# Taking matmul columns alternately from halves and quarters in 13 feature blocks of a feed-forward layer

## The chip, the core and the metric

The kernel runs on one core of a Trainium2 chip. Its engines work side by side, each on a queue of its own: TensorE (PE in the profile; its weight loads are listed apart as PEld) multiplies matrices, VectorE (DVE) and ScalarE (ACT) do elementwise work, GpSimd (POOL) a few small operations, and SyncE (SP) issues the loads of weights. Operands lie in SBUF, sums of matmuls in the eight banks of PSUM, 512 float32 columns each. The metric is the device time of one execution in microseconds (us); lower is better.

## The reference

Two layers, each a mixer followed by a SwiGLU feed-forward part, over 256 tokens with 1024 features, and a norm at the end. The change lies in the feed-forward part of layer 0:

```python
def swiglu(h, w13, w2):
    g, u = jnp.split(h @ w13, 2, axis=-1)
    return ((jax.nn.silu(g) * u) @ w2).astype(h.dtype)

for layer in range(DEPTH):
    y = rms_norm(h, norm_mix[layer])
    ...
    h = h + y
    h = h + swiglu(rms_norm(h, norm_ffn[layer]), ffn_w13[layer], ffn_w2[layer])
```

D_FF is 2816, so that `h @ w13` has 2 x 2816 output features: 22 blocks of 128 for the gate half g and as many for the half u. Inputs and outputs are float32.

## The kernel before

**Precision.** TensorE takes the operands as float32r. To keep the accuracy each operand is split into a high and a low part (`whi`, `wlo` for weights, `xh`, `xl` for activations, `hh`, `hl` for the hidden ones), and every product is three matmuls: high by high, low weights by high, high weights by low. `mm_w` (line 479) issues these three, with 128 x 128 weights as the stationary operand and 256 columns (all tokens) as the moving one, onto the same 256 columns of a PSUM bank. `mm` (line 454) is the helper behind all matmuls but the transposes, so that they all carry line 455 in the profile.

**Layout.** Features stand on the partitions, tokens along them. The activations x of layer 0's feed-forward part are eight pairs of tiles of 128 x 256, one pair per block k of input features.

**The feed-forward part** (`swiglu`, called with layer 0 and the bank group "A", so its sums are `psA`). Blocks 0 to 3 of the output features run together over the input blocks k. Then comes a loop over j from 4 to 21, one output block at a time (lines 997 to 1001):

```python
            b = main_bank(gu)
            for half in range(2):
                for k in range(KT):
                    mm_w(b[:, half * S:half * S + S], piece("ffn_w13", layer, k, half * DFF + P * j, P), x[k],
                         start=(k == 0 and half == 0), stop=(k == KT - 1))
```

The gate half fills columns 0 to 255 of the bank, the u half columns 256 to 511: 2 x 8 x 3 = 48 matmuls of 256 columns. `hidden(j, b)` then queues on VectorE and ScalarE what turns the bank into the hidden block (`sgq`, `u`, `hh`, `hl`), and `down(j - 4, hs)` runs the down projection of an earlier hidden block, 8 x 3 = 24 matmuls onto four banks of group "B" (`psB`), whose moving operand is `hh` and `hl`. So TensorE alternates between 48 matmuls onto `psA` and 24 onto `psB`. The tiles `hh0` and `hl0` take the place of `q1` and `k1` of the recurrence, which are laid out 304 columns wide with pads of 16 columns; the other hidden tiles are 256 wide.

**Weights** arrive by SyncE's loads of 512 KB into `raw`; ScalarE rounds them to `whi` (line 412) and VectorE subtracts to get `wlo` (line 414), each into a ring of six buffers, which come free as TensorE moves on.

**The order** of all engines' instructions is made while the program is built, by `Order`: it keeps a model clock for each engine, `od.main(MM)` advances TensorE's by 109.2 ns for each matmul, and `od.pump()` emits the queued operations that are due. The change leaves these calls as they are.

**The recurrence's level matmuls** of layer 0's mixer (`level` in `Core.scores`) are the place where the kernel before takes moving columns in pieces: of 128 columns of q it takes m, leaves m, and so on, with m of 2, 4, 8 and 16, 64 columns in all, against 128 - m columns of k. They write their columns side by side. `mov,k` are the recurrence's matmuls with 192 columns, taken side by side.

Of the kernel before, what the change touches and what calls it, by code (L numbers as in the profile page):

```python
# [20 lines left out]
KT = D // P  # L21
# [6 lines left out]
SUB = 1024  # L28
FIRST = (512, 512, 512, 512)
LEVELS = (1, 2, 4, 8, 16)  # L30
BUCKET_STARTS = tuple(range(17)) + (21, 27, 35, 46, 59, 77, 99, 128, 166, 216)


# [249 lines left out]
def cv(n, fast=False):  # L283
    return ((n / 2 if fast else n) + 66) / 0.96


def ca(n, ptr=0):
    return n / 1.2 + 93 + 93 * ptr
# [14 lines left out]
def hybrid_trunk(ctx: ExitStack, tc: tile.TileContext, wts, xT, par, gfin, tab, onehot, masks, out):  # L303
# [15 lines left out]
    def new(tag, shape, bufs=1, dt=FT, held=False):  # L319
        return ring(tag, shape, bufs, dt).new(held)  # L320
# [37 lines left out]
    def bank(g, held=False):  # L358
        return rings["ps" + g].new(held)

    def main_bank(g):

        b = bank(g, held=True)
        r = b.ring
        od.need(lambda: od.free_at(r))
        b.tile = r.make()
        r.past.append(b)
        return b
# [7 lines left out]
    def wrote(b):  # L376
        b.writers = [Mark(od.now)]
# [56 lines left out]
    def piece(name, layer, k, c0, n):  # L434
        assert plan[ws["piece"]] == (name, layer, k, c0, n), (plan[ws["piece"]], (name, layer, k, c0, n))
        ws["piece"] += 1
        if ws["col"] == subs[ws["sub"]][2]:
            ws["sub"] += 1
            ws["col"] = 0
            if keep["from"] is None:  # L440
                free_subs(ws["sub"])
        i, c = ws["sub"], ws["col"]
        make_subs(i + NSUB + 4)
        ws["col"] += n
        return Piece(i, c, n)

    def free_subs(upto):
        for j in range(max(0, upto - 12), upto):
            if hi_b[j].held:
                hi_b[j].held = lo_b[j].held = False  # L450
                hi_b[j].readers.append(Mark(od.now))
                lo_b[j].readers.append(Mark(od.now))

    def mm(o, a, b, start=False, stop=False):
        T.matmul(o, a, b, start=start, stop=stop, skip_group_check=True)  # L455
# [20 lines left out]
                b.held = False  # L476
                b.readers.append(Mark(od.now))

    def mm_w(o, w, x, start=False, stop=False):
        mm(o, w.hi, x.hi, start=start)  # L480
        od.main(MM)
        mm(o, w.lo, x.hi)
        od.main(MM)
        mm(o, w.hi, x.lo, stop=stop)
        od.main(MM, 1)
        od.pump()

# [33 lines left out]
    for k0, k1 in [(k, k + 1) for k in range(4)] + [(4, 6), (6, 8)]:  # L521
        od.op("S", 60, lambda k0=k0, k1=k1: nc.sync.dma_start(hT[:, k0:k1, :], xT[:, k0:k1, :]),  # L522
              writes=hb[k0:k1], nbytes=131072 * (k1 - k0), due=8 * k0 - 6)
    NMK = 2 * P + 64 * 2 * len(LEVELS)
    bt = new("bt", [P, NH * S])
# [90 lines left out]
    def out_rows(name, layer, k, us, banks, nk, done):  # L616

        if k == nk - 2:
            return
        ks = (k - 1, k) if k == nk - 1 else (k,)  # L620
        for j in range(KT):
            b, s = banks[j // 2], (j % 2) * S
            for kk in ks:
                mm_w(b[:, s:s + S], piece(name, layer, kk, P * j, P), us[kk], start=(kk == 0 and j % 2 == 0),
                     stop=(kk == nk - 1))
            if k == nk - 1 and j % 2:
                wrote(b)
                done(j // 2)
                b.held = False
        for kk in ks:  # L630
            us[kk].free()
# [21 lines left out]
    def feature_major(name, layer, c0, x, g):  # L653
        b = main_bank(g)
        for k in range(KT):
            mm_w(b[:, :S], piece(name, layer, k, c0, P), x[k], start=(k == 0), stop=(k == KT - 1))
        wrote(b)
        b.held = False
        return b
# [64 lines left out]
    class Core:  # L724
# [91 lines left out]
        def scores(self, due):  # L816
            h, Q, K, mov = self.h, self.Q, self.K, self.mov
            pm = pms[h % 2]
            moff = {m: 2 * P + P * i for i, m in enumerate(LEVELS)}

# [78 lines left out]
    for h in range(NH):  # L899
        c = Core(h)  # L900
# [46 lines left out]
    def swiglu(layer, x, stats, gu, down):  # L947

        hs = {}

        def hidden(j, b):
            gs = new("sgq", [P, S], 3)
            sg = new("u", [P, S], 3)
            due = 6
            od.op("V", cv(S), lambda: V.tensor_tensor(gs.tile, b[:, :S], stats.row.tile, op=OP.mult),  # L955
                  reads=[b, stats.row], alloc=[gs], due=due)
            od.op("A", ca(S), lambda: A.activation(sg.tile, gs.tile, AF.Sigmoid), reads=[gs], alloc=[sg], due=due)  # L957
            od.op("V", cv(S), lambda: V.tensor_tensor(gs.tile, gs.tile, sg.tile, op=OP.mult), reads=[sg], writes=[gs], due=due)
            od.op("V", cv(S), lambda: V.tensor_tensor(sg.tile, b[:, S:], gs.tile, op=OP.mult), reads=[b, gs], writes=[sg],
                  due=due)  # L960
            x = X("h", j % 7)
            hi, lo = x.h, x.l
            od.op("A", ca(S), lambda: A.activation(hi.tile, sg.tile, AF.Copy), reads=[sg], alloc=[hi], due=due + 6)
            od.op("V", cv(S), lambda: V.tensor_tensor(lo.tile, sg.tile, hi.tile.bitcast(FT), op=OP.subtract),
                  reads=[sg, hi], alloc=[lo], due=due + 6)
            hs[j] = x

        bk = [main_bank(gu) for _ in range(4)]
        for k in range(KT - 2):
            w = {}  # L970
            keep["from"] = ws["sub"]
            for j in range(4):
                for half in range(2):
                    w[j, half] = piece("ffn_w13", layer, k, half * DFF + P * j, P)
                    o = bk[j][:, half * S:half * S + S]
                    mm(o, w[j, half].hi, x[k].hi, start=(k == 0 and half == 0))
                    od.main(MM)
                    mm(o, w[j, half].lo, x[k].hi)
                    od.main(MM, .67)
                    od.pump()  # L980
            for j in range(4):
                for half in range(2):
                    mm(bk[j][:, half * S:half * S + S], w[j, half].hi, x[k].lo)
                    od.main(MM, .33)
                od.pump()
            keep["from"] = None
            free_subs(ws["sub"])
        for j in range(4):
            for half in range(2):
                for k in (KT - 2, KT - 1):  # L990
                    mm_w(bk[j][:, half * S:half * S + S], piece("ffn_w13", layer, k, half * DFF + P * j, P), x[k],
                         stop=(k == KT - 1))
            wrote(bk[j])
            hidden(j, bk[j])
            bk[j].held = False
        for j in range(4, FTN):
            b = main_bank(gu)
            for half in range(2):
                for k in range(KT):
                    mm_w(b[:, half * S:half * S + S], piece("ffn_w13", layer, k, half * DFF + P * j, P), x[k],  # L1000
                         start=(k == 0 and half == 0), stop=(k == KT - 1))
            wrote(b)
            hidden(j, b)
            b.held = False
            od.written(stats.row)
            down(j - 4, hs)
        for k in range(KT):
            x[k].free()
        down(FTN - 4, hs, last=True)
# [10 lines left out]

    od.written(sto.row)
    swiglu(0, x1, st1, "A", down0)


# [191 lines left out]
    def down1(k, hs, last=False):  # L1216
# [23 lines left out]
        if not last:  # L1240
            hs[k].free()

    swiglu(1, x3, st3, "B", down1)
    od.flush()


def _constants():
# [3 lines left out]
    for i in range(384):  # L1251
# [3 lines left out]
        else:  # L1255
            onehot[sum(dist >= s for s in BUCKET_STARTS) - 1, i] = 1.0
    s = np.arange(P)[:, None]
    m = [np.tile(np.eye(P, dtype=np.float32), (1, 2))]
    for lv in LEVELS:
        t = np.arange(P).reshape(-1, 2, lv)[:, 1].reshape(1, -1)  # L1260
# [30 lines left out]
```

## Time and profile before

| | |
|---|---|
| time, median of 2 runs | 630.43 us (630.02 to 630.84) |
| span of the profiled execution, first to last instruction (its device time is not listed apart) | 629.2 us |
| weights read from HBM | 109.78 MB, 176 GB/s over the span |
| loop over j of layer 0's feed-forward part, from block 6's first matmul to block 21's | 192.15 to 314.71 us |
| TensorE, VectorE, ScalarE busy in that stretch | 122.56, 77.92, 56.97 us |

In the profile, PE rows are matmuls, and matmuls overlap in the pipeline, so what one costs is the distance between the starts of two that follow each other. A row of the order in time gives the start in us, the length in us, the engine, the line, the operation, out<-in, the stationary operand's shape, the moving one's, and a count. In the table of stretches each engine has its busy time and the number of its instructions, and then come the granted TensorE clock (1.00 is full), the busy share of the DMA engines and what they moved.

### The profile page before, as it was taken

The page shows a single profiled execution, that of the slowest core. Times are in us where ns is not written, and L with a number is a line of the kernel's source. Part 1 is how long each engine was busy: PE and PEld are TensorE (multiplying, and loading weights), DVE is VectorE, ACT ScalarE, POOL GpSimd, SP SyncE. Part 2 cuts the span into 40 slices and gives each one's busy share as a digit, 9 for nine tenths or more (in the row PEclk, how much of TensorE's full clock was granted, in tenths as well). Part 3 has the DMA queues.
Part 4 walks back from the last instruction along what each step waited for, and adds up shares of the span by engine and source line. Part 5 has one row for each costly group of instructions (what it writes and reads, how often), then busy time and mean ns, then how long its engine had stood idle before and what let it go on. Part 6 is the DMA issues. An engine that isn't in the chain of part 4 may idle for free.

```text
span 629.2 us, 12441 instructions
## 1 busy us (share of the span) xinstructions
PE 617.4 (98%) x4848; PEld 594.2 (94%) x4848; DVE 441.0 (70%) x800; ACT 364.2 (58%) x715; POOL 39.2 (6%) x74
## 2 busy tenths in 40 slices
PE   7999999999999999999999999999999999999995
PEld 5899999999999999999998899999899999999994
DVE  5898878877786666666659678866686666666653
ACT  6798888875564444444446566564674444444443
POOL 0132112200400000000000000000100000000003
PEclk9999999999999999999999999999999999999998
DMA  8964443534896666666653564445545665555501
GB/s 273 324 217 136 154 128 123 155 115 134 209 282 200 194 199 198 190 189 198 201 189 116 209 223 160 143 154 182 180 160 197 201 199 197 177 188 176 168 1 67
DMA packets 32135, 111.83 MB, mean 178 GB/s; under 512 B 3835, under 2 KB 4508, under 8 KB 32076
## 3 DMA queue, kind: packets, MB, share of 16 engines
q1 hardware_dynamic: 31052, 108.71, 53.4%
q0 software_dynamic: 448, 1.25, 1.0%
q10 hardware_dynamic: 576, 1.08, 0.6%
q8 instruction: 38, 0.62, 0.4%
q14 instruction: 21, 0.17, 0.1%
HBM read 109.78 MB, written 1.25 MB: 176 GB/s over the span
## 4 chain that ended last, share of the span: by engine, by line
PE 78%; issue 16%; DVE 3%; DMA 1%; ACT 1%; POOL 1%; SPq 0%; ACTq 0%; DVEq 0%; POOLq 0%
PE psB L455 44%; PE psA L455 33%; DMA raw<-in_w_dram 1%; DVE wlo L414 1%; POOL ny L591 1%; DVE xl L541 0%; DVE yt L607 0%; ACT whi L412 0%; DVE hT L609 0%; DVE sqacc L559 0%; PE psB L1146 0%; SPq L401 0%; SPq L522 0%; PE psA L596 0%; DVE raw L1177 0%
## 5 line engine op out<-in xcount | busy, mean ns | idle before, releaser
L414 DVE TENSOR_TENSOR wlo<-raw,whi 128x1024 fp32r<-128x1024 f32 (+1 forms) x206 | 247.8, 1213 | 107.8 <-ACT whi L412 107.4
L412 ACT ACTIVATE whi<-raw 128x1024 fp32r<-128x1024 f32 (+1 forms) x205 | 213.0, 1050 | 145.7 <-issue 66.7
L455 PE MATMUL psB<-xh,whi 128*128 128x256 f32 x608 | 172.6, 287 | 0.0
L455 PE MATMUL psB<-xh,wlo 128*128 128x256 f32 x608 | 167.6, 279 | 0.0
L455 PE MATMUL psB<-xl,whi 128*128 128x256 f32 x608 | 163.3, 279 | 0.0
L455 PE MATMUL psA<-xh,whi 128*128 128x256 f32 x544 | 150.3, 280 | 0.0
L455 PE MATMUL psA<-xh,wlo 128*128 128x256 f32 x544 | 148.8, 277 | 0.0
L455 PE MATMUL psA<-xl,whi 128*128 128x256 f32 x544 | 144.0, 277 | 0.0
L455 PEld LDWEIGHTS psB<-xh,wlo 128*128 128x128 f32 x608 | 114.6, 188 | 0.7
L455 PEld LDWEIGHTS psB<-xh,whi 128*128 128x128 f32 x608 | 114.4, 188 | 0.8
L455 PEld LDWEIGHTS psB<-xl,whi 128*128 128x128 f32 x608 | 112.2, 189 | 0.0
L455 PEld LDWEIGHTS psA<-xh,whi 128*128 128x128 f32 x544 | 102.4, 188 | 0.6 <-issue 0.5
L455 PEld LDWEIGHTS psA<-xh,wlo 128*128 128x128 f32 x544 | 102.2, 188 | 0.0
L455 PEld LDWEIGHTS psA<-xl,whi 128*128 128x128 f32 x544 | 99.2, 188 | 0.0
L455 PE MATMUL psB<-hl,whi 128*128 128x256 f32 x176 | 48.7, 277 | 0.0
L455 PE MATMUL psB<-hh,whi 128*128 128x256 f32 x176 | 48.7, 277 | 0.0
L455 PE MATMUL psB<-hh,wlo 128*128 128x256 f32 x176 | 48.7, 276 | 0.0
L957 ACT ACTIVATE u<-sgq 128x256 f32<-128x256 f32 x44 | 18.0, 410 | 38.9 <-DVE sgq L955 38.7
L455 PE MATMUL psA<-wlo,hh 128*128 128x512 f32 x88 | 34.6, 393 | 0.0
L455 PE MATMUL psA<-whi,hl 128*128 128x512 f32 x88 | 34.5, 392 | 0.0
L455 PE MATMUL psA<-whi,hh 128*128 128x512 f32 x88 | 34.5, 392 | 0.0
L455 PEld LDWEIGHTS psB<-hl,whi 128*128 128x128 f32 x176 | 33.1, 188 | 0.0
(178 smaller groups left out, 793.8 us busy)
## 6 DMA issues: line engine op xcount, KB each, us to landing
raw<-in_w_dram SPq DMA_DIRECT2D x202, 512.0 KB, 4.2
raw<-in_w_dram SPq DMA_DIRECT2D x4, 256.0 KB, 3.3
bt<-scr POOLq DMA_DIRECT2D x8, 128.0 KB, 9.1
hT<-in_x_dram SPq DMA_DIRECT2D x4, 128.0 KB, 5.1
hT<-in_x_dram SPq DMA_DIRECT2D x2, 256.0 KB, 8.1
bt<-in_final_dram ACTq DMA_DIRECT2D x1, 512.0 KB, 5.4
out_dram<-raw ACTq DMA_DIRECT2D x2, 256.0 KB, 2.2
out_dram<-raw SPq DMA_DIRECT2D x2, 256.0 KB, 2.0
```

Source lines behind the costliest of these rows:

```text
L412: od.op("A", ca(n), lambda h=h, r=r, o=o, n=n: A.activation(h[:, :n], r[:, o:o + n], AF.Copy), reads=[r], alloc=[h], due=due)
L414: od.op("V", cv(n), lambda h=h, lo=lo, r=r, o=o, n=n: V.tensor_tensor(lo[:, :n], r[:, o:o + n], h[:, :n].bitcast(FT), op=OP.subtract), rea ...
L455: T.matmul(o, a, b, start=start, stop=stop, skip_group_check=True)
L591: od.op("G", 500, lambda: G.tensor_tensor(y.tile, v.tile, mhalf, op=OP.pow), reads=[v], alloc=[y], due=due)
L957: od.op("A", ca(S), lambda: A.activation(sg.tile, gs.tile, AF.Sigmoid), reads=[gs], alloc=[sg], due=due)
```

## The change

Thirteen of the eighteen blocks of the loop over j, in layer 0 alone, get an order of their columns. `in_order` splits the 256 columns into `a` parts and takes pieces of `c` columns from the parts in turn; it is applied to the moving operand and to the output alike, so that each column's sum lands where it did before. With (2, 16) the columns go 0 to 15, 128 to 143, 16 to 31, 144 to 159 and so on; with (4, 16) a piece comes from each quarter in turn. Blocks 4, 5, 11, 20 and 21 keep the plain order. The branch for "odd" is used by no block.

```diff
+ORDERS = {6: (2, 16), 7: (2, 16), 8: (2, 4), 9: (2, 4), 10: (2, 2), 12: (2, 64), 13: (2, 64), 14: (2, 8), 15: (2, 8),
+          16: (2, 32), 17: (4, 16), 18: (4, 8), 19: (4, 32)}
...
-    def mm_w(o, w, x, start=False, stop=False):
-        mm(o, w.hi, x.hi, start=start)
+    def in_order(t, order):
+
+        if order is None:
+            return t
+        if order == "odd":
+            return t.rearrange("p (b a) -> p a b", a=2)
+        a, c = order
+        return t.rearrange("p (a b c) -> p b a c", a=a, c=c)
+
+    def mm_w(o, w, x, start=False, stop=False, order=None):
+        o = in_order(o, order)
+        mm(o, w.hi, in_order(x.hi, order), start=start)
         od.main(MM)
-        mm(o, w.lo, x.hi)
+        mm(o, w.lo, in_order(x.hi, order))
         od.main(MM)
-        mm(o, w.hi, x.lo, stop=stop)
+        mm(o, w.hi, in_order(x.lo, order), stop=stop)
...
             b = main_bank(gu)
+            order = ORDERS.get(j) if layer == 0 else None
             for half in range(2):
                 for k in range(KT):
                     mm_w(b[:, half * S:half * S + S], piece("ffn_w13", layer, k, half * DFF + P * j, P), x[k],
-                         start=(k == 0 and half == 0), stop=(k == KT - 1))
+                         start=(k == 0 and half == 0), stop=(k == KT - 1), order=order)
```

On TensorE's queue, where block 6 follows the down projection of block 1's hidden features, this stood before (out<-in with buffer numbers, then partitions x columns of the output):

```order
L455 MATMUL psB<-hh_2728,wlo 128x256
L455 MATMUL psB<-hl_2733,whi 128x256
L455 MATMUL psA<-xh_2350,whi 128x256
L455 MATMUL psA<-xh_2350,wlo 128x256
L455 MATMUL psA<-xl_2357,whi 128x256
L455 MATMUL psA<-xh_2352,whi 128x256
```

and this stands there now:

```order
L457 MATMUL psB<-hh_2728,wlo 128x256
L457 MATMUL psB<-hl_2733,whi 128x256
L457 MATMUL psA<-xh_2350,whi 128x8x2x16
L457 MATMUL psA<-xh_2350,wlo 128x8x2x16
L457 MATMUL psA<-xl_2357,whi 128x8x2x16
L457 MATMUL psA<-xh_2352,whi 128x8x2x16
```

The order is the same, and the output's 256 columns have become 8 x 2 pieces of 16. At the end of block 10, the one with the shortest pieces, TensorE's queue read before:

```order
L455 MATMUL psA<-xh_2458,wlo 128x256
L455 MATMUL psA<-xl_2476,whi 128x256
L455 MATMUL psB<-hh_3032,whi 128x256
L455 MATMUL psB<-hh_3032,wlo 128x256
L455 MATMUL psB<-hl_3048,whi 128x256
```

and reads now:

```order
L457 MATMUL psA<-xh_2458,wlo 128x64x2x2
L457 MATMUL psA<-xl_2476,whi 128x64x2x2
L457 MATMUL psB<-hh_3032,whi 128x256
L457 MATMUL psB<-hh_3032,wlo 128x256
L457 MATMUL psB<-hl_3048,whi 128x256
```

Here the block's last matmuls have 64 x 2 pieces of 2 columns, and the down projection behind them is untouched. The queues of VectorE, ScalarE, GpSimd and SyncE hold the same instructions in the same order as before.

## The prediction

> **What bounds the kernel now.** I read the page first: the busy table, the rows of the 40 slices for TensorE and its granted clock, and the shares of the chain that ended last.
>
> ```profile
> span 629.2 us, 12441 instructions
> PE 617.4 (98%) x4848; PEld 594.2 (94%) x4848; DVE 441.0 (70%) x800; ACT 364.2 (58%) x715; POOL 39.2 (6%) x74
> PE   7999999999999999999999999999999999999995
> PEclk9999999999999999999999999999999999999998
> PE 78%; issue 16%; DVE 3%; DMA 1%; ACT 1%; POOL 1%; SPq 0%; ACTq 0%; DVEq 0%; POOLq 0%
> ```
>
> TensorE works in every slice at an undiminished clock, and the chain runs along its matmuls. So the time is the number of matmuls times the interval at which they start. The second view is the table of stretches, over the blocks that the change touches (a row runs from the first gate matmul of a block j to that of the next; the first row is block 6, the second block 7), and the waits between 190 and 310 us.
>
> ```profile
> core 0: us, PE busy (x) PEld busy (x) DVE busy (x) ACT busy (x) POOL busy (x), PEclk, DMA share, GB/s
> 192.15:200.31 8.16, 8.16 (x74) 8.16 (x73) 5.15 (x8) 3.80 (x5) 0.00 (x0) 1.00 0.63 196
> 200.31:208.47 8.16, 8.16 (x74) 8.16 (x73) 5.20 (x8) 3.80 (x5) 0.00 (x0) 1.00 0.62 193
> 290.07:298.37 8.30, 8.30 (x74) 8.30 (x73) 5.34 (x8) 3.79 (x5) 0.00 (x0) 1.00 0.61 193
> 298.37:306.55 8.18, 8.18 (x74) 8.18 (x73) 5.06 (x8) 3.80 (x5) 0.00 (x0) 1.00 0.59 196
> ACT whi L412 <- PE psA L455: 26.3, 16, 1.7
> DVE sgq L955 <- PE psA L455: 5.4, 15, 0.4
> ```
>
> TensorE fills the 8.16 us of a block, VectorE works 5.2 us of it and ScalarE 3.8, the DMA engines 0.6 of it, and it is ScalarE and VectorE that wait for TensorE, not the reverse. Nothing else can become the bound here before TensorE's share shrinks by a third. The third view is the order in time on TensorE: the first matmuls of block 6, its last, and the first of the down projection after it.
>
> ```profile
> 192.15 0.28 PE L455 MATMUL psA<-xh,whi 128*128 128x256 f32 x1
> 192.26 0.28 PE L455 MATMUL psA<-xh,wlo 128*128 128x256 f32 x1
> 192.38 0.28 PE L455 MATMUL psA<-xl,whi 128*128 128x256 f32 x1
> ...
> 197.48 0.28 PE L455 MATMUL psA<-xl,whi 128*128 128x256 f32 x1
> 197.59 0.28 PE L455 MATMUL psB<-hh,whi 128*128 128x256 f32 x1
> ```
>
> The 0.28 us of a row is not its price, since the rows overlap; the distance between starts is. 48 matmuls begin in 197.59 - 192.15 = 5.44 us: **113.3 ns** each. The change touches 13 blocks of 48, so 624 matmuls, which take 624 x 113.3 ns = 70.7 us now, 11% of the span. That is all that can move directly. A result 2% off (12.6 us, about what a measurement of this kernel can tell from no change) needs 12.6 us / 624 = 20 ns more or less for each of them on average, 18% of its interval.
>
> **The change, part by part.** Nothing is added, removed or moved in any queue: the same instructions stand in the same order on every engine, with the same waits, and the DMA issues stay where they are. What is new is the shape of the pattern by which 624 matmuls read their moving columns and write their sums. I count piece starts (256 columns over the piece's length): 16 for pieces of 16, 64 for 4, 128 for 2, 4 for 64, 32 for 8, 8 for 32. Over the blocks this is 2x16 + 2x64 + 128 + 2x4 + 2x32 + 8 + 16 + 32 + 8 = 424, times 48 matmuls = 20,352 piece starts. VectorE reads the finished bank as before, and no weight load changes.
>
> First cost: reading in pieces. The trace of before has such reads: the recurrence's level matmuls take 64 columns of q in pieces of 2, 4, 8 and 16 (their stationary operand has 126, 124, 120 and 112 columns), four records each. I take the distance from their start to the next row's.
>
> ```profile
> 44.07 0.81 PE L455 MATMUL psA<-mov,k 128*128 128x192 f32 x4
> 44.72 0.55 PE L455 MATMUL psA<-q,k 128*126 128x64 f32 x4
> 45.07 0.36 PE L455 MATMUL psB<-xh,whi 128*128 128x256 f32 x1
> ...
> 46.92 0.54 PE L455 MATMUL psA<-q,k 128*124 128x64 f32 x4
> 47.28 0.36 PE L455 MATMUL psB<-xh,whi 128*128 128x256 f32 x1
> ...
> 47.71 0.54 PE L455 MATMUL psA<-q,k 128*120 128x64 f32 x4
> 48.06 0.36 PE L455 MATMUL psB<-xh,whi 128*128 128x256 f32 x1
> ...
> 49.91 0.51 PE L455 MATMUL psA<-q,k 128*112 128x64 f32 x4
> 50.23 0.36 PE L455 MATMUL psB<-xh,whi 128*128 128x256 f32 x1
> ```
>
> That is 0.35, 0.36, 0.35 and 0.32 us for pieces of 2, 4, 8 and 16. Pieces of 2 cost no more than pieces of 4, although they have twice the starts; the shorter 0.32 goes with the narrowest weights. If all of it were the pieces, a start would cost (0.35 - 0.32) us / (4 x (32 - 4)) = 0.27 ns, and the change 20,352 x 0.27 ns = 5.5 us. The other end is zero, and I take zero, because the two finest sizes, which differ most in starts, lie in the wrong order for a cost per start.
>
> Second cost: writing in pieces. Every matmul of before writes its columns side by side, so no row shows it. Below zero it cannot go by itself: a column still has to be written. From above I bound it by a column taking two turns in place of one, which is the interval of a matmul with 512 columns (below, 526.79 - 525.66 = 1.13 us for five of them, 226 ns), or 113 ns more for each of the 624, +70.5 us. Of the two ends I take zero: read side and write side walk the same pattern, and the read side shows nothing.
>
> ```profile
> 519.30 0.28 PE L455 MATMUL psB<-xh,whi 128*128 128x256 f32 x1
> ...
> 524.06 0.39 PE L455 MATMUL psA<-whi,hh 128*128 128x512 f32 x1
> ...
> 525.66 0.39 PE L455 MATMUL psA<-wlo,hh 128*128 128x512 f32 x1
> 525.89 0.39 PE L455 MATMUL psA<-whi,hl 128*128 128x512 f32 x1
> ...
> 526.79 0.28 PE L455 MATMUL psB<-xh,whi 128*128 128x256 f32 x1
> 526.91 0.28 PE L455 MATMUL psB<-xh,wlo 128*128 128x256 f32 x1
> ...
> 529.27 0.28 PE L455 MATMUL psB<-xh,whi 128*128 128x256 f32 x1
> ```
>
> Here a rule speaks against the change. The Trainium skill's "PSUM — Partial Sum Buffer", section "Specifications (TRN2)", gives PSUM 8-byte cachelines and says of them "any non-contiguous AP slows matmuls significantly"; 8 bytes are two float32 columns, so by the line alone pieces of 2 and more would still fill whole lines, and by the sentence every changed matmul would pay. No row here shows either. If the sentence holds, an estimate with twice the write time gives 701 us; if only the line matters, the sum stays.
>
> Third cost: the meeting of the two reads. While a matmul reads its moving columns, the weights of the next are read too (the row of a weight load below starts 0.01 us after the matmul before it in block 6 and lasts 0.19 us), and the interval depends on where the moving tile lies. The down projection of block 14, the same kind of matmul with the same clock, reads the first buffer of the tile hh0 (14 mod 7 is 0), which is laid out with other gaps (it takes q1's place), and starts more slowly:
>
> ```profile
> 192.16 0.19 PEld L455 LDWEIGHTS psA<-xh,wlo 128*128 128x128 f32 x1
> ...
> 296.57 0.28 PE L455 MATMUL psB<-hh,whi 128*128 128x256 f32 x1
> ...
> 298.37 0.29 PE L455 MATMUL psA<-xh,whi 128*128 128x256 f32 x1
> ```
>
> 15 matmuls in 1.80 us are 120.0 ns each; this is the 8.30 us row in the table above. Alternating halves changes which column is read at which moment of the weight load, so a changed block may move to another interval. The slow end is 120.0 ns: 624 x 6.7 ns = +4.2 us. For the fast end I use the row of the 192-column matmuls above: 44.72 - 44.07 = 0.65 us for four, 162.5 ns each; at 113.3 ns per 256 columns 192 would take 85 ns, so I assume that they pass twice (384 columns), which makes 108.3 ns for 256: 624 x -5.0 ns = -3.1 us. I see no reason for either end and take the middle, +0.5 us. If TensorE did gain 0.24 us a block, the cover stays: ScalarE's waits for it alone are 26.3 us over 120 us.
>
> Sum: 0 + 0 + 0.5 = +0.5 us on a span of 629.2, that is 629.7. The page gives the profiled execution's span alone; the two timed runs, 630.02 and 630.84, lie 0.8 and 1.6 us above it, so I add 0.5 to their median: **630.9 us**.
>
> **The rivals.** (1) *Each piece start costs one column's turn*, on the write side, where no row excludes it: 113.3 / 256 = 0.44 ns x 20,352 = 9.0 us, 639.4 us. Against it: the read side's bound of 0.27 ns. (2) *Slower by over 2%*: the write side stalls, by more than 0.62 ns per piece start (12.6 us / 20,352); two turns per start give 648.4 us, and two turns per column wherever a write is split 630.4 + 70.5 = 701 us. For it speaks only that no row shows a split write; if the doubling held for pieces of 2 alone, block 10 would pay 48 x 113 ns = 5.4 us, and that stays within 2%. The Trainium skill's "PSUM — Partial Sum Buffer", "Specifications (TRN2)", would have it at the doubling by its sentence and at nothing by its 8 bytes. (3) *The interval does not come back*: after a changed block the unchanged matmuls keep a slower rhythm. The rows above show that such a rhythm lasts: from 526.79 to 529.27 us 21 matmuls start at 118.1 ns, although the 42 matmuls of the same kind and stage from 519.30 to 524.06 us kept 113.3 ns. Between 192.15 and 333.75 us there are some 1,250 matmuls; at 118 instead of 113.3 ns they would cost 5.9 us, 636.3 us. Against it: after the slow down projection of block 14 the table returns from 8.30 to 8.18 us in the next block. (4) *It helps*: every changed block reaches 108.3 ns, 627.3 us. More than that would need a matmul that streams faster than any row shows. That the change does nothing measurable is no separate rival; it is the middle of my forecast.
>
> **How the numbers follow.** The likeliest case, changed blocks between 108.3 and 120.0 ns and nothing else, holds 627.3 to 634.7 us; I give it 0.66. Rival (3) gets 0.10, rival (1) 0.10, rival (2) 0.11. The last 0.03 lies below 627.3, of which 0.01 is under 617.8, faster by 2%. The range goes from the fast end, 627.3, to rival (1), 639.5: it holds 0.66, the 0.10 of (3) and about half of (1), 0.8. Faster by over 2%: 0.01; slower: rival (2), 0.11; within: 0.88.
>
> **What would show it.** The unchanged blocks 4, 5, 11, 20 and 21 stand between the changed ones and are the measure: the table of stretches, block by block, should read 8.16 us for all, within 7.9 and 8.5. If piece starts cost something, block 10 (128 starts) is the longest, then 8 and 9 (64), then 14, 15 and 18 (32), and 12 and 13 (4) are like 11. If only the halves' meeting with the weight load matters, the order does not follow the number of starts. If a split write costs by the column, all thirteen grow, 12 and 13 too. A rhythm that stays shows as an unchanged block 11 or 20 above 8.16. I am wrong if any changed block exceeds 8.5 us, or if the time goes outside 627.3 to 639.5.

## The result, and the profile after

| | before | changed |
|---|---|---|
| time, median of 2 runs | 630.43 us (630.02 to 630.84) | 637.40 us (636.77 to 638.04) |
| span of the profiled execution | 629.2 us | 635.0 us (its own time 636.77 us) |
| ratio of the times | | 1.0115, 95% interval 1.0082 to 1.0148 |

The changed kernel is 7.0 us slower, 1.15%: a clear difference, within 2%. The page's busy table and the rows of its slices for TensorE and its clock, in the changed kernel:

```profile
span 635.0 us, 12442 instructions
PE 623.4 (98%) x4848; PEld 600.4 (95%) x4848; DVE 440.9 (69%) x800; ACT 364.2 (57%) x715; POOL 41.5 (7%) x74
PE   8999999999999999999999999999999999999995
PEclk9999999999999999999999999999999999999998
```

TensorE is as full as before, at the same clock, with the same 4848 matmuls, and 6.0 us busier. So the matmuls themselves follow each other more slowly. The order in time on TensorE at the start and the end of block 10 (pieces of 2) shows where it is worst:

```profile
225.51 0.33 PE L457 MATMUL psA<-xh,whi 128*128 128x256 f32 x1
225.67 0.34 PE L457 MATMUL psA<-xh,wlo 128*128 128x256 f32 x1
225.84 0.34 PE L457 MATMUL psA<-xl,whi 128*128 128x256 f32 x1
...
233.66 0.29 PE L457 MATMUL psB<-hh,whi 128*128 128x256 f32 x1
```

Starts lie 0.17 us apart where they lay 0.113 apart before. The table of stretches of the changed kernel follows, cut this time to the 48 gate and u matmuls of a block (blocks 6, 8, 10, 11, 12, 14, 18 and 20); its last row is the tail of 120 down-projection matmuls behind block 21, which took 13.60 us before. The length of a stretch, the number behind its bounds, divided by 48 is the interval.

```profile
core 0: us, PE busy (x) PEld busy (x) DVE busy (x) ACT busy (x) POOL busy (x), PEclk, DMA share, GB/s
190.78:196.56 5.78, 5.78 (x51) 5.78 (x49) 3.35 (x5) 2.43 (x3) 0.00 (x0) 1.00 0.55 184
207.88:213.95 6.07, 6.07 (x50) 6.07 (x49) 3.38 (x5) 2.45 (x3) 0.00 (x0) 1.00 0.52 173
225.51:233.66 8.15, 8.15 (x50) 8.15 (x49) 3.38 (x5) 2.44 (x3) 0.00 (x0) 1.00 0.48 138
236.41:241.84 5.43, 5.43 (x50) 5.43 (x49) 3.38 (x5) 2.44 (x3) 0.00 (x0) 1.00 0.58 194
244.56:250.00 5.44, 5.44 (x50) 5.44 (x49) 3.40 (x5) 2.43 (x3) 0.00 (x0) 1.00 0.58 192
260.88:266.80 5.92, 5.92 (x51) 5.92 (x49) 3.40 (x5) 2.43 (x3) 0.00 (x0) 1.00 0.56 180
295.19:300.83 5.64, 5.64 (x51) 5.64 (x49) 3.38 (x5) 2.43 (x3) 0.00 (x0) 1.00 0.58 189
312.29:317.94 5.65, 5.65 (x50) 5.65 (x49) 3.29 (x5) 2.43 (x3) 0.00 (x0) 1.00 0.55 181
326.42:340.55 14.13, 14.13 (x122) 14.13 (x121) 9.51 (x14) 7.17 (x10) 0.00 (x0) 1.00 0.58 187
```

The plain block 11 still takes 5.43 us, and so does block 12 with its pieces of 64. Block 10 takes 8.15, and the blocks with pieces of 4 to 32 between 5.64 and 6.07. Two rows are a surprise: block 20 and the tail are not changed, and yet slower than before. VectorE's and ScalarE's work is what it was.

Against 5.44 us a block, the account of this stage is: block 10, 2.71 us; blocks 8 and 9 (6.07 each), 1.26; the eight blocks with pieces of 8 to 32 (46.20 in all against 43.52), 2.68; blocks 12 and 13 nothing. That is 6.65 us. The two views below give the whole stage, from block 6 to the end of the tail, and what lies behind it, first before, then changed.

```profile
192.15:333.75 141.60, 141.60 (x1250) 141.60 (x1249) 90.61 (x123) 66.36 (x88) 0.00 (x0) 1.00 0.61 194
333.75:629.20 295.45, 287.07 (x2126) 270.97 (x2124) 198.43 (x350) 155.68 (x264) 8.53 (x6) 0.99 0.50 163
```

```profile
190.78:340.55 149.77, 149.77 (x1250) 149.77 (x1249) 90.83 (x124) 66.62 (x88) 0.00 (x0) 1.00 0.56 183
340.55:635.00 294.45, 285.99 (x2126) 270.09 (x2124) 198.27 (x349) 155.60 (x264) 8.54 (x6) 0.99 0.50 163
```

The stage lost 149.77 - 141.60 = 8.17 us: 6.65 in the changed matmuls and 1.52 in unchanged ones (0.42 in blocks 20 and 21, 0.53 in the tail, the rest in down projections between the blocks). The part behind it, with the same instructions, gained 1.0 us, and block 6 began 1.4 us earlier in this execution, at a point ahead of which nothing differs. 8.2 - 1.0 - 1.4 = 5.8 us, the difference of the two spans. Neither gain is shown to be the change's doing: in the kernel below that only writes in pieces block 6 begins 1.2 us earlier too, and the last experiment comes back to the gain behind the stage.

### The profile page after: what moved, and what is told of

It reads as the page before. It is cut to its first block, busy times and chain, and to the rows that moved or that the text cites. A ratio compares the mean times of both kernels' runs of the same rounds, so it can differ in the third digit from the quotient of the medians.

```text
span 635.0 us, 12442 instructions
## 1 busy us (share of the span) xinstructions
PE 623.4 (98%) x4848; PEld 600.4 (95%) x4848; DVE 440.9 (69%) x800; ACT 364.2 (57%) x715; POOL 41.5 (7%) x74
## 4 chain that ended last, share of the span: by engine, by line
PE 77%; issue 16%; DVE 3%; POOL 1%; DMA 1%; ACT 1%; SPq 0%; DVEq 0%; ACTq 0%; POOLq 0%
PE psB L457 42%; PE psA L457 34%; DVE wlo L416 1%; POOL ny L603 1%; DMA raw<-in_w_dram 1%; DVE xl L553 1%; DVE sqacc L571 1%; DVE yt L619 0%; ACT whi L414 0%; DVE hT L621 0%; PE psB L1159 0%; SPq L403 0%; SPq L534 0%; PE psA L608 0%; DVE sqacc L592 0%
## 5 line engine op out<-in xcount | busy, mean ns | idle before, releaser
L457 PE MATMUL psA<-xh,whi 128*128 128x256 f32 x544 | 152.6, 284 | 0.0
L457 PE MATMUL psA<-xh,wlo 128*128 128x256 f32 x544 | 151.1, 281 | 0.0
L457 PE MATMUL psA<-xl,whi 128*128 128x256 f32 x544 | 146.3, 281 | 0.0
L457 PEld LDWEIGHTS psB<-xh,whi 128*128 128x128 f32 x608 | 114.4, 188 | 0.8
```

## The experiments

**Read or write.** Two kernels each keep one half of the change. The first reads in pieces and writes side by side:

```diff
     def mm_w(o, w, x, start=False, stop=False, order=None):
-        o = in_order(o, order)
         mm(o, w.hi, in_order(x.hi, order), start=start)
```

> Only the moving columns are read in the changed order; the sums are written side by side, so in the thirteen blocks the tokens of the hidden features stand in another order and the output differs. If the cost lies in the read (the moving read meeting the weight read), the intervals of the changed kernel come back: block 10 at 170 ns, blocks 8 and 9 at 126, 14 and 15 at 123, 6 and 7 at 120, and the time is about 637. If it lies in the write, every block stays at 113.3 ns and the time is about 630. If both sides pay, block 10 lies between, about 140.

The second writes in pieces and reads side by side:

```diff
         o = in_order(o, order)
-        mm(o, w.hi, in_order(x.hi, order), start=start)
+        mm(o, w.hi, x.hi, start=start)
         od.main(MM)
-        mm(o, w.lo, in_order(x.hi, order))
+        mm(o, w.lo, x.hi)
         od.main(MM)
-        mm(o, w.hi, in_order(x.lo, order), stop=stop)
+        mm(o, w.hi, x.lo, stop=stop)
```

> The mirror: moving columns are read side by side, only the sums are written in the changed order; again the tokens of the thirteen blocks stand in another order. If the write pays, block 10 is at 170 ns, blocks 8 and 9 at 126, 14 and 15 at 123, and the time is about 637; if the read pays, all blocks stay at 113.3 ns and the time is about 630. If what counts is that the pattern has pieces at all (instruction handling), this run and the other one both show the full cost.

Measured: 638.12 us for the read alone, 630.56 for the write alone, beside 630.27 for the kernel before. The table of stretches of the kernel that only reads in pieces, blocks 8, 10 and 14:

```profile
208.15:214.22 6.07, 6.07 (x51) 6.07 (x49) 3.38 (x5) 2.44 (x3) 0.00 (x0) 1.00 0.54 173
225.78:233.93 8.15, 8.15 (x51) 8.15 (x50) 3.37 (x5) 2.44 (x3) 0.00 (x0) 1.00 0.44 140
261.15:267.06 5.91, 5.91 (x50) 5.91 (x49) 3.39 (x5) 2.42 (x3) 0.00 (x0) 1.00 0.56 180
```

and of the one that only writes in pieces, the same blocks:

```profile
207.25:212.69 5.44, 5.44 (x51) 5.44 (x49) 3.39 (x5) 2.43 (x3) 0.00 (x0) 1.00 0.61 194
223.57:229.01 5.44, 5.44 (x51) 5.44 (x49) 3.39 (x5) 2.43 (x3) 0.00 (x0) 1.00 0.63 193
256.21:261.65 5.44, 5.44 (x51) 5.44 (x49) 3.40 (x5) 2.43 (x3) 0.00 (x0) 1.00 0.62 193
```

The read carries the whole cost, block by block to the hundredth of a microsecond; writing sums in pieces of 2 or more costs nothing.

**Block 10 by itself.** It goes back to the plain order:

```diff
-ORDERS = {..., 9: (2, 4), 10: (2, 2), 12: (2, 64), ...}
+ORDERS = {..., 9: (2, 4), 12: (2, 64), ...}
```

> Block 10 (pieces of 2) goes back to the plain order, the other twelve blocks keep theirs. By the intervals of the changed kernel block 10 costs 48 x 56.5 ns = 2.7 us, so 637.4 - 2.7 = 634.7, ratio to the kernel before 1.007. If the cost were a fixed one per piece start (128 of 424), 637.4 - 7.0 x 128 / 424 = 635.3. If a slow rhythm left behind by block 10 made the rest slow, the rest falls back too and the time is under 632.

Measured: 634.51 us, ratio to the kernel before 1.0078 (1.0052 to 1.0104). Block 10 is 2.7 to 2.9 us of the 7.0, as its interval says. A slow rhythm left behind by block 10, with a time under 632, is out; the time alone does not exclude 635.3, but the next run does.

**Short pieces, or alternating halves?** Same lengths and number of pieces, taken from neighbours:

```diff
-        return t.rearrange("p (a b c) -> p b a c", a=a, c=c)
+        return t.rearrange("p (b a c) -> p a b c", a=a, c=c)
```

> The same blocks take pieces of the same length and number, on both sides, but skipping neighbours (0, 1, 4, 5, 8, 9 and so on, then 2, 3, 6, 7) in place of alternating between halves. If the length of a piece sets the cost, block 10 stays near 170 ns and 8 and 9 near 126. If the alternation between halves does it (two reads that keep step with the weight load), block 10 falls to 113 to 125 ns. Blocks 12 and 13 (64) stay at 113 to 120 either way.

Measured: 638.61 us. Blocks 8 and 10 of this kernel:

```profile
208.32:213.98 5.66, 5.66 (x51) 5.66 (x50) 3.39 (x5) 2.42 (x3) 0.00 (x0) 1.00 0.55 185
225.08:236.09 11.01, 11.01 (x50) 9.99 (x49) 3.39 (x5) 2.42 (x3) 0.00 (x0) 1.00 0.44 143
```

Neither expectation fits. Block 10 did not fall and did not stay: it rose to 11.01 / 48 = 229.4 ns, twice the plain interval, while pieces of 4 fell from 126.5 to 117.9. A price per piece start (rival 1 of the prediction) is out, since the starts are the same in number. What fits pieces of 2: a column costs nothing by itself, a fetch of 16 aligned bytes (4 columns) does. With neighbours every such part is fetched twice, 128 fetches in place of 64, and the second comes half a matmul later; with halves the second use comes two pieces later.

**The 16 bytes tested.** Seven blocks use 240 columns from a start that is or isn't a multiple of 4 columns:

```diff
+ORDERS = {7: (2, 4, 0), 9: (2, 4, 2), 11: (2, 4, 4), 13: (2, 8, 0), 15: (2, 8, 2), 17: (1, 240, 0), 19: (1, 240, 2)}
...
+        a, c, off = order
+        return t[:, off:off + 240].rearrange("p (a b c) -> p b a c", a=a, c=c)
...
-                         start=(k == 0 and half == 0), stop=(k == KT - 1), order=order)
+                         start=(k == 0 and half == 0), stop=(k == KT - 1), order=order if k else None)
```

> Seven blocks leave 16 of the 256 columns out of the products of input blocks 1 to 7 and read the other 240 from column 0, 2 or 4 on, in halves with pieces of 4 (blocks 7, 9, 11 start at 0, 2, 4), of 8 (13 and 15 start at 0 and 2) and side by side (17 and 19 start at 0 and 2). Theory A, a fetch covers 16 aligned bytes (4 columns): pieces of 4 that start at column 2 need two fetches and block 9 goes far above block 7, towards 150 to 200 ns, while block 11 equals block 7 (about 119 ns, 240 / 256 of 126); block 15 is above block 13 by a fifth or more; 17 and 19 are alike near 107 to 110 ns. Theory B, only length and number of the pieces count: 7, 9 and 11 are alike, 13 and 15 too.

Measured, in the stretches of 21 such matmuls of the gate half, blocks 7, 9, 11, 13, 15, 17 and 19 in turn:

```profile
200.74:203.16 2.42, 2.42 (x24) 2.42 (x22) 1.71 (x3) 1.28 (x2) 0.00 (x0) 1.00 0.61 208
217.16:220.45 3.29, 3.29 (x23) 3.29 (x22) 1.86 (x3) 1.28 (x2) 0.00 (x0) 1.00 0.61 184
235.41:237.82 2.41, 2.41 (x23) 2.41 (x22) 1.71 (x3) 1.28 (x2) 0.00 (x0) 1.00 0.67 221
251.82:254.21 2.39, 2.39 (x24) 2.39 (x23) 1.69 (x3) 1.28 (x2) 0.00 (x0) 1.00 0.65 219
268.60:272.10 3.50, 3.50 (x23) 3.50 (x22) 1.74 (x3) 1.26 (x2) 0.00 (x0) 1.00 0.58 173
287.16:289.51 2.35, 2.35 (x23) 2.35 (x22) 1.65 (x3) 1.28 (x2) 0.00 (x0) 1.00 0.71 223
303.62:305.99 2.37, 2.37 (x23) 2.37 (x22) 1.53 (x3) 1.25 (x2) 0.00 (x0) 1.00 0.65 221
```

Starting 8 bytes off raises pieces of 4 from 115 to 157 ns (2.42 and 3.29 us over 21) and pieces of 8 from 114 to 167, while the same pieces 16 bytes off (third row) are back at 115, and columns side by side hardly notice. Length and number are equal in each pair, so theory B is out and theory A's 16-byte parts are borne out. One size was missed: 240 columns side by side took 112 and 113 ns, not 107 to 110, so the interval doesn't fall in step with the columns here, and no run shows what holds it. And pieces of 8 that start 8 bytes off touch 90 parts and cost more than pieces of 4, which touch 120; a single price per part doesn't give that. The last section comes back to it.

**Other strides.**

```diff
+ORDERS = {8: (4, 2), 10: (8, 2), 12: (8, 4), 14: (4, 4), 16: (8, 8), 18: (16, 4), 20: (8, 16)}
```

> Other orders in blocks 8 to 20: quarters and eighths with pieces of 2 (blocks 8 and 10), eighths with 4 (12), quarters with 4 (14), eighths with 8 (16), sixteenths with 4 (18), eighths with 16 (20). Theory A (a fetch of 4 columns, and a part fetched shortly before is used again, which makes halves with 2 cost 170 and neighbours with 2, which come back late, 229): blocks 8 and 10 come back to a 16-byte part after 4 and 8 pieces and lie near 229. Theory B (a fixed price per piece start): blocks 8 and 10 are at 170 like block 10 of the change. By both, 4 and more columns stay between 113 and 127 ns.

Measured: 643.14 us; the rows are blocks 8, 10, 12, 14 and 18.

```profile
207.60:218.49 10.89, 10.89 (x50) 9.95 (x49) 3.39 (x5) 2.43 (x3) 0.00 (x0) 1.00 0.47 147
229.41:240.46 11.05, 11.05 (x51) 9.87 (x49) 3.39 (x5) 2.43 (x3) 0.00 (x0) 1.00 0.41 142
251.38:257.45 6.07, 6.07 (x51) 6.07 (x49) 3.39 (x5) 2.43 (x3) 0.00 (x0) 1.00 0.51 173
268.35:274.91 6.56, 6.56 (x51) 6.56 (x49) 3.40 (x5) 2.47 (x3) 0.00 (x0) 1.00 0.47 162
302.44:307.93 5.49, 5.49 (x51) 5.49 (x50) 3.39 (x5) 2.43 (x3) 0.00 (x0) 1.00 0.60 194
```

Pieces of 2 whose 16 bytes come back after four or eight pieces cost 227 and 230 ns: no reuse, as theory A said. But pieces of 4, which always fill their 16 bytes, spread from 114.4 ns (sixteenths, 64 bytes from one piece to the next) over 126.5 (eighths, 128 bytes) to 136.7 (quarters, 256 bytes), above the expected 127. So the distance between successive parts matters too. No run here separates why.

**Where the tiles lie.** The change as it is, with the moving tiles 64 bytes lower, and then, in another kernel, with the moving tiles in place and the weights 64 bytes higher:

```diff
-        sb.tile([P, 48], FT, name="gap")
+        sb.tile([P, 32], FT, name="gap")
```

> The change as it is, but the pad ahead of the moving tiles is 32 columns in place of 48, which moves all activations 64 bytes against the weights. If the few ns of pieces of 4 to 32 come from the moving read meeting the weight read, the plain blocks and those blocks get other intervals, by 2 ns or more, while block 10 stays within 160 to 180. If they belong to the pieces alone, every block keeps its interval within 1 ns.

```diff
-        sb.tile([P, 96], FT, name="lead")
+        sb.tile([P, 112], FT, name="lead")
...
-        sb.tile([P, 48], FT, name="gap")
+        sb.tile([P, 32], FT, name="gap")
```

> The change as it is, but the weight tiles move 64 bytes up and the moving tiles stay where they are, so that the distance between both is the one of the run with the moving tiles 64 bytes down. If the distance between the two reads sets the interval of plain blocks, they take 118.8 ns as in that run and the time is near 650. If the moving tiles' own place does, they keep 113.3 ns and the time is near 637.

Measured: 650.56 and 652.88 us, against 637.4. Blocks 10, 11 and 14 with the moving tiles moved:

```profile
230.31:238.52 8.21, 8.21 (x51) 8.21 (x49) 3.23 (x5) 2.44 (x3) 0.00 (x0) 1.00 0.48 138
241.37:247.07 5.70, 5.70 (x51) 5.70 (x49) 3.27 (x5) 2.43 (x3) 0.00 (x0) 1.00 0.58 187
267.00:272.92 5.92, 5.92 (x50) 5.92 (x49) 3.26 (x5) 2.43 (x3) 0.00 (x0) 1.00 0.54 180
```

and with the weights moved:

```profile
230.54:238.75 8.21, 8.21 (x51) 8.21 (x49) 3.24 (x5) 2.44 (x3) 0.00 (x0) 1.00 0.41 139
241.60:247.30 5.70, 5.70 (x51) 5.70 (x49) 3.27 (x5) 2.43 (x3) 0.00 (x0) 1.00 0.58 187
267.23:273.15 5.92, 5.92 (x50) 5.92 (x49) 3.26 (x5) 2.43 (x3) 0.00 (x0) 1.00 0.56 180
```

The two agree row by row, so it is the distance between moving tile and weights that sets the interval of a plain block: 5.70 / 48 = 118.8 ns at this distance, 113.3 at the kernel's own. Pieces of 2 and of 8 hardly change (8.15 to 8.21 us, 5.92 both times), and pieces of 16 from halves neither (120 ns both times), while pieces of 4 go from 126.5 to 129.4 ns and pieces of 64 move with the plain order, from 5.44 to 5.70 us. So neither expectation for the moved tiles came out whole. One reading is that the plain order profits from the kernel's own distance and shorter pieces lose that profit. It is a reading, and not the whole: pieces of 4 and 8 are slower than plain blocks at either distance.

**Ending a slow rhythm.** In layer 1 of the kernel before, block 12 and all that follow run at 117.9 ns, and so they do in all eight traces of kernels that have its tile places and leave that block plain. No block of layer 0 is changed; block 12 of layer 1 gets halves with pieces of 16:

```diff
+ORDERS = {12: (2, 16)}
...
+            order = ORDERS.get(j) if layer == 1 else None
```

> No order in layer 0; in layer 1 block 12 alone, the first at 117.8 ns there, takes halves with pieces of 16. If the slow rhythm is a state that a different block can end, blocks 13 to 21 go back to 113.9 ns and the time falls by up to 9 x 48 x 4 ns = 1.7 us, to 628.7. If the rhythm is set by where the tiles lie, they stay at 117.8 and the time is 630.5.

Measured: 627.82 us against 629.98, ratio 0.9963 (0.9950 to 0.9977). Blocks 12, 13 and 21 of layer 1 in this kernel, and then 13 and 21 in the kernel before:

```profile
525.78:531.54 5.76, 5.76 (x50) 5.76 (x48) 3.75 (x4) 2.67 (x3) 0.00 (x0) 1.00 0.54 175
534.30:539.76 5.46, 5.46 (x49) 5.46 (x48) 3.72 (x4) 2.65 (x3) 0.00 (x0) 1.00 0.48 158
600.00:605.47 5.47, 5.47 (x49) 5.46 (x48) 3.75 (x4) 2.67 (x3) 0.00 (x0) 1.00 0.01 3
```

```profile
535.21:540.87 5.66, 5.66 (x50) 5.65 (x48) 3.72 (x4) 2.64 (x3) 0.00 (x0) 1.00 0.48 132
602.57:608.23 5.66, 5.66 (x50) 5.65 (x48) 3.73 (x4) 2.64 (x3) 0.00 (x0) 1.00 0.01 3
```

The matmuls of block 13 are identical in both kernels, tiles and places included. So the slow rhythm is a state that lasts, and a block of another shape ended it for good. It is worth 1.7 us: from block 12's start to the end the two traces take 629.2 - 526.79 = 102.4 and 626.5 - 525.78 = 100.7 us. The nine blocks behind block 12 gain 9 x 0.2 = 1.8, block 12 itself loses 0.1, and the down projections between them change by 0.01 us each. What else parts the two traces lies ahead of block 12, where the kernels are the same.

Are three matmuls enough? Pieces of 8 in the first three matmuls of that block, and in the first three of the attention's output projection:

```diff
+KICK = (2, 8)
...
+                         order=KICK if layer == 1 and j == 12 and half == 0 and k == 0 else None)
...
+                     stop=(kk == nk - 1), order=KICK if name == "moba_w_out" and (j, kk) == (0, 0) else None)
```

> No order in layer 0; pieces of 8 from halves in two places only, three matmuls each: the first of block 12 in layer 1, and the first of the attention's output projection, whose stage ran at 118.6 ns. If three matmuls are enough to end the slow rhythm, blocks 12 to 21 of layer 1 take 113.9 ns (-1.9 us, and -0.9 us for their down projections) and the output projection falls to 114 (-0.6 us): about 627.2. If a rhythm only ends after a whole block, the time is 630.

Measured: 627.73 us against 629.61, ratio 0.9971 (0.9954 to 0.9988). The three matmuls, the 45 behind them, and block 13:

```profile
525.07:525.43 0.36, 0.36 (x4) 0.36 (x3) 0.17 (x1) 0.36 (x1) 0.00 (x0) 1.00 0.75 307
525.43:530.55 5.12, 5.12 (x47) 5.12 (x46) 3.59 (x3) 2.31 (x3) 0.00 (x0) 1.00 0.47 144
533.30:538.77 5.47, 5.47 (x50) 5.47 (x48) 3.74 (x4) 2.66 (x3) 0.00 (x0) 1.00 0.49 145
```

The 45 run at 113.8 ns at once. Three matmuls do as much as a block, and cost 0.02 us more than three plain ones. The 0.9 us expected in the down projections did not come: one takes 2.74 us where it took 2.76. The output projection's 105 matmuls ran at 114.3 ns here, but so they did in the kernel with block 12 of layer 1 changed, where no matmul ahead of them differs from the kernel before; the rows are the kernel before, the changed one, and that one:

```profile
422.36:434.81 12.45, 12.45 (x109) 12.45 (x107) 7.08 (x9) 6.19 (x9) 0.00 (x0) 1.00 0.54 172
428.81:440.81 12.00, 12.00 (x108) 12.00 (x107) 7.06 (x9) 6.09 (x9) 0.00 (x0) 1.00 0.54 178
421.52:433.52 12.00, 12.00 (x109) 12.00 (x107) 7.05 (x9) 6.09 (x9) 0.00 (x0) 1.00 0.54 178
```

Of the ten traces with these tile places only that of the kernel before has 12.45 us. The 0.45 us is a difference between executions, and not a gain of these three matmuls. The two kernels that end the slow rhythm are faster than the kernel before and the changed one; the intervals don't tell the two apart.

## Why the prediction was right or wrong

The measured 637.4 us lies in the range of 627.3 to 639.5, and on the side of the point, but the point moved by +0.5 us and the kernel by +7.0. The likeliest outcome, within 2%, came; the sum was wrong. That the range held was in part luck: its upper end came from rival (1), whose mechanism was wrong, and the case given 0.66, changed blocks between 108.3 and 120.0 ns and nothing else (up to 634.6 us by its own terms, not 634.7), did not happen. The prediction's own sign of being wrong, a changed block above 8.5 us, did: block 10 with the down projection behind it took 236.41 - 225.51 = 10.9 us.

- *What bounds the kernel, and what can move:* right. The stage's whole loss lies in TensorE's intervals, no other engine became the bound, and 6.65 us of it are in the 624 matmuls.
- *Second cost, the write:* zero was taken and zero it is, though the reason given, that the read side shows nothing, fell with the first cost; the kernel that only writes in pieces keeps 113.3 ns in all changed blocks but block 19, whose 5.46 us stand in the kernel before too. So the sentence of the Trainium skill's "PSUM — Partial Sum Buffer", "Specifications (TRN2)", that any non-contiguous pattern slows matmuls significantly, does not hold for pieces of 2 columns and more; its 8-byte line is consistent with what was measured.
- *First cost, the read:* this step failed. It took zero "because the two finest sizes, which differ most in starts, lie in the wrong order for a cost per start". The cost isn't per start but per 16-byte part, and pieces of 2 pay it: 2.7 us in block 10. The row that misled is that of the recurrence's float32 matmuls: 0.35 us for four records of 64 columns is 1.4 ns per column, against 113.3 / 256 = 0.44 ns in the changed blocks. Reads that are wanted three times more slowly have slack that can hide the price; I took the row over without comparing the rates. Pieces of 2 of the same pattern doubled the interval when tried in these blocks. At that price, 113.3 / 64 = 1.8 ns a part, the 32 parts of a record (two columns out of each) would take an estimated 57 ns, and the records start 0.35 us / 4 = 88 ns apart, so there is room for it. That the slack is the reason is argued, not run.
- *Third cost, the meeting of the reads:* the mechanism was right in part and the term mis-sized: "I see no reason for either end and take the middle, +0.5 us". Ten blocks went to 117.5 to 126.5 ns, 1.26 + 2.68 = 3.9 us, near the slow end of +4.2 that was reckoned for all thirteen. There was a reason for that end: the plain blocks already stood at a good distance, and the 120.0 ns row showed what is lost without it. But 120.0 ns is no bound: pieces of 4 and 8 took 126.5 and 123.3, and 129.4 and 123.3 when the distance changed. That the distance between the tiles sets the interval is shown for plain blocks alone; what sets it for short pieces of whole parts stays open.
- *Rival (3), a rhythm that stays:* it happened, on top of slower changed blocks: 1.5 us in unchanged matmuls. The return after block 14's down projection, the argument against it, was one case; behind block 19 the rhythm stayed until the stage's end, and it did so too in the kernel that only reads in pieces and in the one without block 10's pieces. Of the rivals' times its 636.3 us lies nearest to the measured one, but it has 5.9 us in unchanged matmuls where 1.5 were measured.
- *Rival (1), a column's turn per start:* its 639.4 us came within 2.0 us of the time, for a wrong reason. Equal starts gave 170 and 229 ns, and block 18 with 32 starts was faster (5.64 / 48, 117.5 ns) than block 6 with 16 (120.4).
- *Not foreseen:* the 1.0 us gained behind the stage. Of this, 0.45 us lie in the 105 plain matmuls of the output projection, which took 12.45 us before and 12.00 after. The change isn't the reason, since the same instructions took 12.00 us in another execution (the rows stand with the last experiment). What decides the rhythm there stays open.

## What to carry to other kernels

The columns of a matmul's sums may be written in another order, in pieces of 2 and more, at no cost seen here. The moving operand should be read in aligned parts of at least 16 bytes; a read of 8 bytes at a time can double the interval of a float32r matmul. Where TensorE is the bound, list the start-to-start interval block by block: unchanged instructions at two intervals (113 and 118 ns here) mean that tile distances or a lasting rhythm are at work, and three matmuls of another shape may be worth 2 us. Before a row of another kind of matmul is used as a price, compare its time per column with that of the place where it is to hold.

## What the runs showed of the hardware

- The moving read is paid by 16-byte parts: 64 parts 113.3 ns, 128 parts 227 to 230 ns. A second visit to a part has two prices. Where it comes four or more fetches later, it adds 1.8 to 1.9 ns, as much as a new part (113.3 / 64 = 1.8): neighbours, quarters and eighths with pieces of 2, and pieces of 8 that start 8 bytes off (28 second visits, 164 to 167 ns). Where it comes two or three fetches later, it adds 0.7 to 0.9 ns: halves with pieces of 2 (64 second visits, 169.8 ns) and pieces of 4 that start 8 bytes off (58, 157 to 160 ns). These prices are worked out: the interval above that of the plain order, or of the same pieces in their place, divided by the number of second visits. That the first fetch is still at hand for so long fits this, and isn't shown apart.
- For full parts the distance to the next matters, at the kernel's own tile places: 114.4 ns at 64 bytes, 117.9 at 32, 126.5 at 128, 126.5 at 512, 136.7 at 256.
- The interval of a plain float32r matmul with 256 columns depends on the distance between moving tile and weights: 64 bytes make 113.3 or 118.8 ns, and 13.2 and 15.5 us over the whole kernel (one execution of each variant).
- The interval has memory: the same matmuls on the same tiles keep 113.8 or 117.9 ns (5.46 and 5.66 us a block) for the last nine blocks of layer 1, depending on what ran ahead of them. The output projection's 105 matmuls took 118.6 ns in one trace and 114.3 in nine, so in places the rhythm also differs from one execution to the next.
